# Seven block products instead of eight, also in the down projection of the feed-forward layers

## The chip, the cores and the metric

The kernel runs on one core of one Trainium2 chip. The metric is the device time of one launch in microseconds (us), as the median of several runs. Lower is better.

## The reference, cut to what matters

The program is a two-layer decoder trunk on 256 tokens of width 2048, all in float32. The change touches only the feed-forward part, which each of the two layers has once:

```python
D_MODEL = 2048; SEQ = 256; FFN_HIDDEN = 5632
def swiglu(xn, w_gu, w_down):          # xn (256, 2048), w_gu (2048, 11264), w_down (5632, 2048)
    g, u = jnp.split(xn @ w_gu, 2, axis=-1)
    return (jax.nn.silu(g) * u) @ w_down
...
h = h + swiglu(rms_norm(h, ffn_norm_g[layer]), ffn_w_gu[layer], ffn_w_down[layer])
```

## The kernel before

**Numbers.** TensorE multiplies in a reduced float32 format. So every operand is kept as two tiles, a rounded `hi` and the rest `lo`, and every product of two blocks is three matmuls: x-hi by w-hi, x-hi by w-lo, x-lo by w-hi. A weight block comes from HBM as a `raw` tile. ScalarE (ACT) casts it to `hi`, VectorE (DVE) subtracts and gives `lo`. This is done by the class `WeightStream`: one call of `ws.next()` hands out the unit that TensorE (PE) multiplies now, emits the split of the unit two places ahead, and the loads of the three units after that. There are three buffers of `raw`, three of `hi` and three of `lo`. SyncE (SP) issues the loads.

**Units.** A unit is 128 x 2048 weights. In the gate and up projection a unit is two row blocks (128 inputs each) by two column blocks of 512, one of gate and one of up; eight units in a row (`kp` 0 to 7) make one pass over the 2048 inputs, for 512 hidden columns. In the down projection a unit is four row blocks by one column block of 512, multiplied by `x_stationary`. Either way a unit of the plain kind ("eight") is 8 block products of 128 x 128 by 128 x 512, which with three matmuls each is 24 matmuls for both halves of the tokens.

**Seven products.** In a gate and up pass the units `kp` 2, 4 and 6 (`SEVEN`) are done by a Strassen-like scheme. A unit is a 2 by 2 matrix of weight blocks, and the tokens and inputs that it meets are a 2 by 2 matrix of 128 x 128 blocks. Sums and differences of blocks on both sides make the product in 7 block products, so 21 matmuls. The price is on the other engines. On the weights (`split_blocks`): one cast and one subtraction of 1536 columns instead of 2048, four sums of 512 columns in place (L184 to L187), and a second split of all four sums into `th` and `tl`. There is one buffer of `th` and of `tl`. On the inputs (`forms`): sums of blocks of x, made once per layer, since the same x meets all gate and up columns. On the output: four products are gathered in four PSUM banks `pb` over the three units; after the last of them DVE joins them with four additions (L707).

**Accumulators.** PSUM has two accumulators `acc` of two banks each, and four single banks. A gate and up pass takes both accumulators, and all four banks from `kp` 2 to 6. The next pass may write its first accumulator when DVE has added the old one into `gate` (L711). In the down projection one pass (512 output columns) takes one accumulator, so two passes alternate.

**Order.** The 5632 hidden columns are worked in three parts of 16, 16 and 12 blocks of 128 (`FFN_PARTS`). In each part, a gate and up pass for every 512 hidden columns, silu and product, and then the transposition of the result into `hT`: eight PE transposes, put into `hT` as hi and lo. That work is queued with `later.put(1, ...)`, so it lands behind the first unit of the next pass. After the gate and up passes of a part come its four down passes (512 output columns each), added into the residual stream `h` (L734). Each engine has a queue that it works off in order; the place of each instruction in it is fixed when the kernel is built.

In the text below, B0 to B7 are the eight units of a gate and up pass, and D0, D1, ... the units of a down pass.

Of the kernel before, what the change touches and what calls it, by code (L numbers as in the profile page):

```python
# [47 lines left out]
SEVEN = (2, 4, 6)  # L48

# [172 lines left out]
def kernel(ctx, tc, consts, x, attn_norm_g, ffn_norm_g, a_w_qkv, a_w_o, kv_norm_g,  # L222
# [411 lines left out]
    def ffn(xT, rstd, finish):  # L634

        with tc.tile_pool(name="ffn", bufs=1) as fp:
# [9 lines left out]
            forms = fp.tile([P, len(SEVEN), 2, 4, P], F32R, name="forms")  # L646

            def scaled(kp):

                x2 = xT[:, 2 * kp:2 * kp + 2, :].rearrange("p k (h s) -> p k h s", s=S)  # L650
                by = row["R"].unsqueeze(1).unsqueeze(1).broadcast_to([P, 2, 2, S])
                nc.vector.tensor_tensor(out=x2, in0=x2.bitcast(F32), in1=by, op=ALU.mult)
                if kp not in SEVEN:
                    return
                f = tmp.tile([P, 2, S], F32, tag="t1", name="f")
                nc.vector.tensor_tensor(out=f, in0=x2[:, :, 0, :].bitcast(F32), in1=x2[:, :, 1, :].bitcast(F32),
                                        op=ALU.add)
                (a11, a21), (a12, a22) = [[f[:, k, t * P:(t + 1) * P] for t in range(NT)] for k in range(2)]
                g = tmp.tile([P, 4, P], F32, tag="t1", name="g")
                for i, x, y, op in ((0, a21, a22, ALU.add), (1, g[:, 0], a11, ALU.subtract),  # L660
                                    (2, a11, a21, ALU.subtract), (3, a12, g[:, 1], ALU.subtract)):
                    nc.vector.tensor_tensor(out=g[:, i], in0=x, in1=y, op=op)
                d = forms[:, SEVEN.index(kp)]
                put_split(d[:, 0], d[:, 1], g)

            def mixed(seven, gate, up):
# [3 lines left out]
                ga, ua = acc_tile(), acc_tile()  # L670
# [8 lines left out]
                for kp in range(KD // 2):  # L679
                    w = ws.next()  # L680
                    x = lambda t, kk: [xT[:, 2 * kp + kk, o + t * P:o + (t + 1) * P] for o in (0, S)]
                    if seven and kp in SEVEN:
                        i = SEVEN.index(kp)
                        st, sp = i == 0, i == len(SEVEN) - 1
                        if st:
                            pb = [bank() for _ in range(4)]
                        y = lambda j: [forms[:, i, h, j, :] for h in range(2)]
                        mul(pb[0], x(0, 0), w[:2], 1, st, sp)
                        mul(ga[:, 0], x(0, 1), w[:2], 3, False, False)
                        mul(ua[:, 0], y(3), w[:2], 2, False, False)  # L690
                        mul(ga[:, 1], x(1, 1), w[2:], 3, False, False)
# [3 lines left out]
                    else:  # L695
                        st, sp = kp == 0, kp == KD // 2 - 1
                        for acc, n in ((ga, 1), (ua, 0)):
# [4 lines left out]
                    if seven and kp == SEVEN[-1]:  # L702
                        u2 = fp.tile([P, 512], F32, tag="u2", name="u2")
                        nc.scalar.copy(out=gate[:, 0], in_=pb[0])
                        for o, x_, y_ in ((u2, pb[2], gate[:, 0]), (gate[:, 1], pb[3], u2),
                                          (up[:, 0], pb[1], u2), (up[:, 1], pb[1], gate[:, 1])):
                            nc.vector.tensor_tensor(out=o, in0=x_, in1=y_, op=ALU.add)  # L707
                if not seven:
                    return ga, ua
                for acc, d in ((ga, gate), (ua, up)):  # L710
                    nc.vector.tensor_tensor(out=d, in0=acc, in1=d, op=ALU.add)  # L711
                return gate, up

            for part, (k0, n) in enumerate(FFN_PARTS):
                last = part == len(FFN_PARTS) - 1
                hT = big_tile([P, 16, 2 * S], F32R, "hT")
                for j in range(0, n, 4):
                    gate, up = [fp.tile([P, NT, 512], F32, tag=m, name=m) for m in ("gate", "up")]
# [4 lines left out]
                    g, u = mixed(not first, gate, up)  # L723
# [3 lines left out]
                    for t in range(NT):  # L727
                        nc.vector.scalar_tensor_tensor(out=up[:, t], in0=u[:, t], scalar=sc_[:, t:t + 1],
                                                       in1=gate[:, t], op0=ALU.mult, op1=ALU.mult)
                    later.put(1, lambda j=j, up=up, hT=hT:  # L730
                              transposed([up[:, t, :] for t in range(NT)], hT, j, None))

                def add(acc, c, t):
                    nc.vector.tensor_tensor(out=chunk(t, c), in0=acc[:, t, :], in1=chunk(t, c), op=ALU.add)  # L734
                    if last:
                        finish(c, t)

                for c in range(4):
# [201 lines left out]
```

## Time and profile before

| | |
|---|---|
| median of 3 runs | 2680.39 us (2678.89 to 2680.82) |
| the profiled execution's own time | 2679.5 us |
| its span, first to last instruction | 2677.7 us |
| TensorE busy | 2661.3 us, 12986 matmuls and transposes |
| VectorE busy | 1915.4 us |
| ScalarE busy | 1264.4 us |
| HBM read | 491.57 MB, 184 GB/s over the span |

The profile lists for each engine the instructions with start and duration, what they waited for, and the chain of work that ended last. A matmul's listed duration overlaps with the next one's; how often one starts tells the rate. The same holds for VectorE in a smaller measure: back-to-back instructions start a little before the one ahead is listed as ended, so the work of a queue is summed by the distance of starts.

### The profile page before, as it was taken

What the parts mean: (1) busy time and instruction counts of PE and PEld (TensorE: products, weight loads), DVE (VectorE), ACT (ScalarE), POOL (GpSimd) and SP (SyncE); (2) the same over time, 40 slices, a digit from 0 to 9 for tenths busy, and PEclk for the clock granted to TensorE, in tenths of its full rate; (3) what the DMA queues carried; (4) which work ended last, traced back from release to release, by engine and by line L of the source; (5) the groups of instructions that cost most, each with busy time, mean ns of one, the idle gap of its engine ahead of it and who ended that gap; (6) DMA issues with size and microseconds to landing.
All of it is one profiled execution on the core that took longest, in us unless ns stands there. A gap on an engine that the chain in (4) does not pass through costs nothing.

```text
span 2677.7 us, 32660 instructions
## 1 busy us (share of the span) xinstructions
PE 2661.3 (99%) x12986; PEld 2236.9 (84%) x12986; DVE 1915.4 (72%) x2584; ACT 1264.4 (47%) x1603; POOL 5.5 (0%) x12
## 2 busy tenths in 40 slices
PE   9999999999999999999999999999999999999998
PEld 7888888888888888888888888888888888888887
DVE  5676577477467668966995796588578848984985
ACT  5444444444444445544553454565445534543553
POOL 0000000000000000000000000000000000000000
PEclk9999999999999999999999999999999999999999
DMA  7545555555555555565565655544555665655564
GB/s 272 189 160 171 189 165 168 186 173 173 173 183 164 195 182 189 189 204 189 189 219 190 204 180 197 161 140 146 174 173 189 205 198 179 219 190 194 191 217 138
DMA packets 302712, 495.78 MB, mean 185 GB/s; under 512 B 12680, under 2 KB 115808, under 8 KB 302176
## 3 DMA queue, kind: packets, MB, share of 16 engines
q1 hardware_dynamic: 301936, 492.64, 55.4%
q8 instruction: 101, 1.65, 0.3%
q10 hardware_dynamic: 624, 1.07, 0.1%
q14 instruction: 51, 0.42, 0.0%
HBM read 491.57 MB, written 2.10 MB: 184 GB/s over the span
## 4 chain that ended last, share of the span: by engine, by line
PE 95%; DVE 2%; DMA 1%; ACT 1%; issue 1%; SPq 0%; POOL 0%; POOLq 0%; DVEq 0%; ACTq 0%
PE acc L444 14%; PE acc L464 12%; PE acc L463 12%; PE acc L465 12%; PE acc L675 9%; PE acc L676 9%; PE acc L677 9%; PE acc L447 7%; PE bank L676 2%; PE bank L675 2%; PE bank L677 2%; PE bank L398 1%; PE bank L559 1%; DMA raw<-in_ffn_w_gu_dram 1%; PE bank L514 1%
## 5 line engine op out<-in xcount | busy, mean ns | idle before, releaser
L157 DVE TENSOR_TENSOR lo<-raw,hi 128x1024 fp32r<-128x1024 f32 (+2 forms) x578 | 667.5, 1179 | 464.2 <-ACT hi L156 447.9
L156 ACT CAST hi<-raw 128x1024 fp32r<-128x1024 f32 (+2 forms) x578 | 561.6, 1017 | 728.0 <-PE acc L465 312.1
L166 ACT CAST hi<-raw 128x1024 fp32r<-128x1024 f32 (+1 forms) x292 | 323.3, 1139 | 317.8 <-PE acc L677 96.3
L167 DVE TENSOR_TENSOR lo<-raw,hi 128x1024 fp32r<-128x1024 f32 (+1 forms) x292 | 383.4, 1330 | 83.5 <-ACT hi L166 82.8
L675 PE MATMUL acc<-hi,xT_f 128*128 128x512 f32 x988 | 387.2, 392 | 1.7 <-DVE gate L711 1.6
L676 PE MATMUL acc<-lo,xT_f 128*128 128x512 f32 x988 | 385.3, 390 | 0.0
L677 PE MATMUL acc<-hi,xT_f 128*128 128x512 f32 x988 | 385.2, 390 | 0.0
L444 PE MATMUL acc<-xT_a,hi 128*128 128x512 f32 x1536 | 379.3, 395 | 0.0
L444 PEld LDWEIGHTS acc<-xT_a,hi 128*128 128x128 f32 x1536 | 281.5, 188 | 53.8
L463 PE MATMUL acc<-hi,hT 128*128 128x512 f32 x704 | 274.7, 390 | 0.0
L465 PE MATMUL acc<-hi,hT 128*128 128x512 f32 x704 | 274.0, 389 | 0.0
L464 PE MATMUL acc<-lo,hT 128*128 128x512 f32 x704 | 274.0, 389 | 0.0
L675 PEld LDWEIGHTS acc<-hi,xT_f 128*128 128x128 f32 x988 | 185.5, 188 | 42.5 <-issue 2.9
L677 PEld LDWEIGHTS acc<-hi,xT_f 128*128 128x128 f32 x988 | 185.5, 188 | 39.3
L676 PEld LDWEIGHTS acc<-lo,xT_f 128*128 128x128 f32 x988 | 185.5, 188 | 38.4
L447 PEld LDWEIGHTS acc<-xT_a,lo 128*128 128x128 f32 x1536 | 196.9, 191 | 7.6
L447 PE MATMUL acc<-xT_a,lo 128*128 128x256 f32 x1536 | 199.2, 283 | 0.0
L166 ACT CAST th<-raw 128x1024 fp32r<-128x1024 f32 x120 | 121.8, 1049 | 73.1 <-DVE raw L186 64.6
L463 PEld LDWEIGHTS acc<-hi,hT 128*128 128x128 f32 x704 | 132.2, 188 | 27.6 <-issue 0.2
L465 PEld LDWEIGHTS acc<-hi,hT 128*128 128x128 f32 x704 | 132.1, 188 | 27.6
L464 PEld LDWEIGHTS acc<-lo,hT 128*128 128x128 f32 x704 | 132.2, 188 | 26.9
L464 PE MATMUL acc<-lo,xT_a 128*128 128x512 f32 x384 | 150.1, 391 | 0.8 <-DVE lo L157 0.6
(222 smaller groups left out, 3539.9 us busy)
## 6 DMA issues: line engine op xcount, KB each, us to landing
raw<-in_ffn_w_gu_dram SPq DMA_DIRECT2D x352, 512.0 KB, 4.5
raw<-in_a_w_qkv_dram SPq DMA_DIRECT2D x143, 1024.0 KB, 4.8
raw<-in_ffn_w_down_dram SPq DMA_DIRECT2D x88, 1024.0 KB, 5.1
raw<-in_a_w_o_dram SPq DMA_DIRECT2D x16, 1024.0 KB, 5.1
raw<-in_b_w_o_dram SPq DMA_DIRECT2D x16, 1024.0 KB, 5.0
raw<-in_b_w_kv_b_dram SPq DMA_DIRECT2D x8, 1024.0 KB, 5.2
raw<-in_b_w_q_b_dram SPq DMA_DIRECT2D x8, 768.0 KB, 4.8
raw<-in_b_w_q_a_dram SPq DMA_DIRECT2D x4, 1024.0 KB, 5.1
```

Of the source, the lines that this page charges most:

```text
L156: nc.scalar.copy(out=h, in_=src)
L157: nc.vector.tensor_tensor(out=l, in0=src, in1=h.bitcast(F32), op=ALU.subtract)
L166: self.nc.scalar.copy(out=hi, in_=src)
L167: self.nc.vector.tensor_tensor(out=lo, in0=src, in1=hi.bitcast(F32), op=ALU.subtract)
L444: mm(out=acc[:, i, :], lhsT=sl(hi, kk), rhs=xT[:, k0 + kk, :], start=first and kk == 0, stop=False)
L447: mm(out=acc[:, i, 0:S], lhsT=sl(lo, kk), rhs=xT[:, k0 + kk, 0:S], start=False, stop=last and kk == nk - 1)
L463: mm(out=acc[:, t, :ncol], lhsT=xh, rhs=rhs(hi, kk), start=st, stop=False)
L464: mm(out=acc[:, t, :ncol], lhsT=xh, rhs=rhs(lo, kk), start=False, stop=False)
L465: mm(out=acc[:, t, :ncol], lhsT=xl, rhs=rhs(hi, kk), start=False, stop=sp)
L675: mm(out=out, lhsT=xh, rhs=wh, start=st, stop=False)
L676: mm(out=out, lhsT=xh, rhs=wl, start=False, stop=False)
L677: mm(out=out, lhsT=xl, rhs=wh, start=False, stop=sp)
```

## The change

The seven-product scheme is now used in the down projection too. Two down passes are joined into one over 1024 output columns, whose units are two row blocks by two column blocks, like those of gate and up. In the two parts of 16 blocks this is done for all four passes (two joined passes of 8 units, seven-product units 2 and 5); in the last part, of 12 blocks, for the first 1024 columns (one joined pass of 6 units, seven-product units 2 and 4), while its last two passes stay as they were. That makes 4 + 4 + 2 = 10 seven-product units per layer, 20 in all.

The gate and up loop is generalised: `mixed` takes the input tile, the list of seven-product units and the sums. `sums` makes the block sums of the inputs; for the down projection it runs on `hT`, behind the transposition that completes the blocks concerned, into a new tile `forms_h`. To make room, `forms` keeps three of four sums; the fourth is written over a block of x that the scheme doesn't read. `joined` adds the joined products into `h`, and each accumulator is then added into `h` on its own.

```diff
+SEVEN_DOWN = {16: (2, 5), 12: (2, 4)}
...
-            for c in range(0, D, 512):
+            v = ffn_w_down[layer].rearrange("(k p) c -> p k c", p=P)
+            last = k0 + n == KF
+            for c in range(0, 1024 if last else D, 1024):
+                for kp in range(n // 2):
+                    blocks = [v[:, k0 + 2 * kp:k0 + 2 * kp + 2, b:b + 512] for b in (c, c + 512)]
+                    units.append((blocks, None, "seven" if kp in SEVEN_DOWN[n] else "eight"))
+            for c in range(1024 if last else D, D, 512):
                 for k in range(k0, k0 + n, 4):
                     add_unit(ffn_w_down[layer], k, 4, c, 512)
...
-            forms = fp.tile([P, len(SEVEN), 2, 4, P], F32R, name="forms")
+            forms = fp.tile([P, len(SEVEN), 2, 3, P], F32R, name="forms")
+            forms_h = fp.tile([P, 2, 2, 4, P], F32R, name="forms_h")
+            def sums(x, kp, d):
+                x2 = x[:, 2 * kp:2 * kp + 2, :].bitcast(F32)
+                f = tmp.tile([P, 2, S], F32, tag="t1", name="f")
+                nc.vector.tensor_tensor(out=f, in0=x2[:, :, 0:S], in1=x2[:, :, S:2 * S], op=ALU.add)
+                (a11, a21), (a12, a22) = [[f[:, k, t * P:(t + 1) * P] for t in range(NT)] for k in range(2)]
+                g = tmp.tile([P, 4, P], F32, tag="t1", name="g")
+                for i, x_, y_, op in ((0, a21, a22, ALU.add), (1, g[:, 0], a11, ALU.subtract),
+                                      (2, a11, a21, ALU.subtract), (3, a12, g[:, 1], ALU.subtract)):
+                    nc.vector.tensor_tensor(out=g[:, i], in0=x_, in1=y_, op=op)
+                if d.shape[2] == 3:
+                    put_split(x[:, 2 * kp, P:S], x[:, 2 * kp, S + P:2 * S], g[:, 0])
+                    g = g[:, 1:]
+                put_split(d[:, 0], d[:, 1], g)
...
-            def mixed(seven, gate, up):
+            def mixed(X, pairs, seven, sums_of, left, right, joined=None):
...
-                    later.put(1, lambda j=j, up=up, hT=hT:
-                              transposed([up[:, t, :] for t in range(NT)], hT, j, None))
+                    def turned(j=j, up=up, hT=hT, seven=SEVEN_DOWN[n]):
+                        transposed([up[:, t, :] for t in range(NT)], hT, j, None)
+                        for kp in (j // 2, j // 2 + 1):
+                            if kp in seven:
+                                sums(hT, kp, forms_h[:, seven.index(kp)])
+                    later.put(1, turned)
+                for c in range(0, 2 if last else 4, 2):
+                    left, right = pair_tiles()
+                    cols = [h[:, :, (c + i) * 512:(c + i + 1) * 512] for i in range(2)]
+                    def joined(cols=cols, parts=(left, right)):
+                        for d, p in zip(cols, parts):
+                            nc.vector.tensor_tensor(out=d, in0=p, in1=d, op=ALU.add)
+                    accs = mixed(hT, n // 2, SEVEN_DOWN[n], forms_h, left, right, joined)
+                    for i, acc in enumerate(accs):
+                        for t in range(NT):
+                            nc.vector.tensor_tensor(out=chunk(t, c + i), in0=acc[:, t, :], in1=chunk(t, c + i),
+                                                    op=ALU.add)
...
-                for c in range(4):
+                for c in range(2 if last else 4, 4):
```

How the queues change is seen best on VectorE, at three places. Names carry a running number of the tile; `lo` and `tl` rows are the second halves of weight splits, `raw` rows the four weight sums of a seven-product unit.

**Place 1: the end of the third part's first down pass** (first layer). Before, on VectorE: the additions into `h` are from an accumulator that alternates with another, and stand between weight splits.

```order
L157 TENSOR_TENSOR lo_12183<-raw_12068,hi_12182 128x1024
L817 MEMSET qz01_13087 64x256
L816 MEMSET qz10_13088 64x256
L817 MEMSET qz11_13089 64x256
L157 TENSOR_TENSOR lo_12215<-raw_12103,hi_12214 128x1024 x2
L734 TENSOR_TENSOR h_7143<-acc_12135,h_7143 128x512 x2
L157 TENSOR_TENSOR lo_12256<-raw_12142,hi_12255 128x1024 x2
```

After, on VectorE: from the join of D4 (the last seven-product unit) to the end of D5 (the last unit of the joined pass).

```order
L158 TENSOR_TENSOR lo_12494<-raw_12394,hi_12493 128x1024 x2
L724 TENSOR_TENSOR u2_12522<-bank_12438,gate_12320 128x512
L158 TENSOR_TENSOR lo_12531<-raw_12434,hi_12530 128x1024
L724 TENSOR_TENSOR gate_12320<-bank_12439,u2_12522 128x512
L724 TENSOR_TENSOR up_12321<-bank_12437,u2_12522 128x512
L724 TENSOR_TENSOR up_12321<-bank_12437,gate_12320 128x512
L766 TENSOR_TENSOR h_7143<-gate_12320,h_7143 128x2x512
L766 TENSOR_TENSOR h_7143<-up_12321,h_7143 128x2x512
L158 TENSOR_TENSOR lo_12531<-raw_12434,hi_12530 128x1024
L771 TENSOR_TENSOR h_7143<-acc_12322,h_7143 128x512 x2
L771 TENSOR_TENSOR h_7143<-acc_12323,h_7143 128x512 x2
```

The rows L771 on `acc_12322` free the accumulator that TensorE's next pass writes first; they now stand behind the join, two additions of 1024 columns and two halves of splits.

**Place 2: a gate and up pass whose `hT` blocks need sums** (the third pass of the first part, first layer), from the `hT` rows to the weight sums of B4. Before, on VectorE:

```order
L374 TENSOR_TENSOR hT_7627<-bank_8325,hT_7627 128x2x256
L167 TENSOR_TENSOR lo_8333<-raw_8204,hi_8332 128x1024
L167 TENSOR_TENSOR lo_8366<-raw_8240,hi_8365 128x1536
L184 TENSOR_TENSOR raw_8240<-raw_8240 128x512
L185 TENSOR_TENSOR raw_8240<-raw_8240 128x512
L167 TENSOR_TENSOR lo_8408<-raw_8291,hi_8407 128x1024
L186 TENSOR_TENSOR raw_8240<-raw_8240 128x512
```

After, on VectorE:

```order
L381 TENSOR_TENSOR hT_7628<-bank_8332,hT_7628 128x2x256
L662 TENSOR_TENSOR f_8339<-hT_7628 128x512
L168 TENSOR_TENSOR lo_8349<-raw_8211,hi_8348 128x1024
L667 TENSOR_TENSOR g_8341<-f_8339 128x128 x2
L667 TENSOR_TENSOR g_8341<-g_8341,f_8339 128x128
L168 TENSOR_TENSOR lo_8382<-raw_8247,hi_8381 128x1536
L667 TENSOR_TENSOR g_8341<-f_8339,g_8341 128x128
L185 TENSOR_TENSOR raw_8247<-raw_8247 128x512
L168 TENSOR_TENSOR lo_8424<-raw_8298,hi_8423 128x1024
L381 TENSOR_TENSOR forms_h_7627<-g_8341,forms_h_7627 128x512
L186 TENSOR_TENSOR raw_8247<-raw_8247 128x512
L168 TENSOR_TENSOR lo_8424<-raw_8298,hi_8423 128x1024
```

Six instructions of the sums (one `f`, four `g`, one `forms_h`) stand between the splits of B3, B4 and B5.

**Place 3: the end of a gate and up pass** (the last of the third part, first layer, where B6 is the last seven-product unit), on VectorE. Before:

```order
L157 TENSOR_TENSOR lo_12098<-raw_12007,hi_12097 128x1024
L707 TENSOR_TENSOR u2_12091<-bank_11938,gate_11827 128x512
L157 TENSOR_TENSOR lo_12098<-raw_12007,hi_12097 128x1024
L707 TENSOR_TENSOR gate_11827<-bank_11939,u2_12091 128x512
L707 TENSOR_TENSOR up_11828<-bank_11937,u2_12091 128x512
L707 TENSOR_TENSOR up_11828<-bank_11937,gate_11827 128x512
L711 TENSOR_TENSOR gate_11827<-acc_11829,gate_11827 128x1024
```

After, on VectorE, at the same place:

```order
L168 TENSOR_TENSOR lo_12246<-raw_12147,hi_12245 128x1024 x2
L724 TENSOR_TENSOR u2_12275<-bank_12118,gate_11998 128x512
L168 TENSOR_TENSOR lo_12282<-raw_12188,hi_12281 128x1024
L724 TENSOR_TENSOR gate_11998<-bank_12119,u2_12275 128x512
L724 TENSOR_TENSOR up_11999<-bank_12117,u2_12275 128x512
L724 TENSOR_TENSOR up_11999<-bank_12117,gate_11998 128x512
L168 TENSOR_TENSOR lo_12282<-raw_12188,hi_12281 128x1024
L744 TENSOR_TENSOR gate_11998<-acc_12000,gate_11998 128x1024
```

One half of a split more stands between the first join row and the addition that frees the first accumulator. This order is found at 4 of the 20 ends of such passes, twice in each layer; at 2 more, the first such end of each layer, both halves stand between the last join row and that addition; at the other 14 the order is that of before.

More of the change, by code (lines that the diff above doesn't have):

```diff
@@ L652, in scaled @@
                 nc.vector.tensor_tensor(out=x2, in0=x2.bitcast(F32), in1=by, op=ALU.mult)
[L653 to L664, printed above, removed]
-            def mixed(seven, gate, up):
-                ga, ua = acc_tile(), acc_tile()
+                if kp in SEVEN:
+                    sums(xT, kp, forms[:, SEVEN.index(kp)])
+            def mixed(X, pairs, seven, sums_of, left, right, joined=None):
+                la, ra = acc_tile(), acc_tile()
                 pb = None
@@ L677, in mul @@
                     mm(out=out, lhsT=xl, rhs=wh, start=False, stop=sp)
[L679 removed]
+                for kp in range(pairs):
                     w = ws.next()
[L681 to L684, printed above, removed]
+                    x = lambda t, kk: [X[:, 2 * kp + kk, o + t * P:o + (t + 1) * P] for o in (0, S)]
+                    if kp in seven:
+                        i = seven.index(kp)
+                        st, sp = i == 0, i == len(seven) - 1
                         if st:
                             pb = [bank() for _ in range(4)]
[L687 removed]
+                        o4 = sums_of.shape[3] - 4
+                        y = lambda j: x(1, 0) if j + o4 < 0 else [sums_of[:, i, h, j + o4, :] for h in range(2)]
                         mul(pb[0], x(0, 0), w[:2], 1, st, sp)
[L689 to L691 removed]
+                        mul(la[:, 0], x(0, 1), w[:2], 3, False, False)
+                        mul(ra[:, 0], y(3), w[:2], 2, False, False)
+                        mul(la[:, 1], x(1, 1), w[2:], 3, False, False)
                         mul(pb[1], y(0), w[2:], 0, st, sp)
@@ L695, in mixed @@
                     else:
-                        st, sp = kp == 0, kp == KD // 2 - 1
-                        for acc, n in ((ga, 1), (ua, 0)):
+                        st, sp = kp == 0, kp == pairs - 1
+                        for acc, n in ((la, 1), (ra, 0)):
                             for t in range(NT):
@@ L701, in mixed, with pair_tiles @@
                     later.tick()
-                    if seven and kp == SEVEN[-1]:
+                    if seven and kp == seven[-1]:
                         u2 = fp.tile([P, 512], F32, tag="u2", name="u2")
-                        nc.scalar.copy(out=gate[:, 0], in_=pb[0])
-                        for o, x_, y_ in ((u2, pb[2], gate[:, 0]), (gate[:, 1], pb[3], u2),
-                                          (up[:, 0], pb[1], u2), (up[:, 1], pb[1], gate[:, 1])):
+                        nc.scalar.copy(out=left[:, 0], in_=pb[0])
+                        for o, x_, y_ in ((u2, pb[2], left[:, 0]), (left[:, 1], pb[3], u2),
+                                          (right[:, 0], pb[1], u2), (right[:, 1], pb[1], left[:, 1])):
                             nc.vector.tensor_tensor(out=o, in0=x_, in1=y_, op=ALU.add)
[L708 to L712, printed above, removed]
+                        if joined:
+                            joined()
+                return la, ra
+            def pair_tiles():
+                return [fp.tile([P, NT, 512], F32, tag=m, name=m) for m in ("gate", "up")]
             for part, (k0, n) in enumerate(FFN_PARTS):
@@ L717, in ffn @@
                 for j in range(0, n, 4):
-                    gate, up = [fp.tile([P, NT, 512], F32, tag=m, name=m) for m in ("gate", "up")]
+                    gate, up = pair_tiles()
                     first = k0 + j == 0
@@ L722, in ffn @@
                             later.put(kp + 3, lambda kp=kp: scaled(kp))
-                    g, u = mixed(not first, gate, up)
+                    g, u = mixed(xT, KD // 2, () if first else SEVEN, forms, gate, up)
+                    if not first:
+                        for acc, d in ((g, gate), (u, up)):
+                            nc.vector.tensor_tensor(out=d, in0=acc, in1=d, op=ALU.add)
+                        g, u = gate, up
                     sc_ = rstd if first else rem
```

6 lines of the change are left out of this document (4 added, 2 removed).

## The prediction

> **What bounds the kernel.** I read the page's busy shares first, then the slices, the chain of work that ended last, and a table of stages.
>
> ```profile
> span 2677.7 us, 32660 instructions
> PE 2661.3 (99%) x12986; PEld 2236.9 (84%) x12986; DVE 1915.4 (72%) x2584; ACT 1264.4 (47%) x1603; POOL 5.5 (0%) x12
> ...
> DVE  5676577477467668966995796588578848984985
> ...
> PEclk9999999999999999999999999999999999999999
> ...
> PE 95%; DVE 2%; DMA 1%; ACT 1%; issue 1%; SPq 0%; POOL 0%; POOLq 0%; DVEq 0%; ACTq 0%
> ```
>
> TensorE is busy 99% of the span at full clock and carries 95% of the chain: a matmul that goes away is time won, as long as no one else is late. VectorE's 72% is an average: the slices reach 9. The table of stages shows which those are (columns: stretch, length, then busy us of PE, PEld, DVE, ACT, POOL).
>
> ```profile
> 1151.50:1240.00 88.50, 88.50 (x396) 73.37 (x395) 45.58 (x45) 34.23 (x35) 0.00 (x0) 1.00 0.57 186
> ...
> 1283.00:1326.00 43.00, 43.00 (x194) 35.46 (x193) 39.54 (x43) 23.05 (x24) 0.00 (x0) 1.00 0.58 196
> ```
>
> The first is the down stage of part one: VectorE works 45.6 of 88.5 us. The second is one gate and up pass with three seven-product units: VectorE works 39.5 of 43. So the change buys TensorE time with VectorE time, and part of the bill (the sums on `hT`) comes due in the passes where VectorE has 8% left.
>
> **Gain.** Starts of units on TensorE: B3, B4, B5 of one pass; then the first row and the end of 15 units of a down stage.
>
> ```profile
> 1296.79 0.39 PE L675 MATMUL acc<-hi,xT_f 128*128 128x512 f32 x1
> 1302.25 0.39 PE L675 MATMUL bank<-hi,xT_f 128*128 128x512 f32 x1
> 1307.08 0.39 PE L675 MATMUL acc<-hi,xT_f 128*128 128x512 f32 x1
> ...
> 1156.73 0.48 PE L463 MATMUL acc<-hi,hT 128*128 128x512 f32 x1
> ...
> 1238.44 0.39 PE L675 MATMUL acc<-hi,xT_f 128*128 128x512 f32 x1
> ```
>
> A plain unit takes 1302.25 - 1296.79 = 5.46 us, a seven-product unit 1307.08 - 1302.25 = 4.83, a down unit (1238.44 - 1156.73)/15 = 5.45. Rearranging a down unit keeps its 24 matmuls, so it costs TensorE nothing; each of 20 seven-product units saves 5.45 - 4.83 = 0.62 us. Gain: **-12.4 us** if nothing waits.
>
> **Place 1, the end of the third part's joined pass (2 times).** TensorE's next pass needs the first accumulator. The same join is in the trace, at the end of a gate and up pass: B7 starts at 1317.36, the next pass at 1322.83.
>
> ```profile
> 1317.36 0.39 PE L675 MATMUL acc<-hi,xT_f 128*128 128x512 f32 x1
> ...
> 1322.83 0.39 PE L675 MATMUL acc<-hi,xT_f 128*128 128x512 f32 x1
> ```
>
> VectorE meanwhile (in brackets: idle before it and who ended that):
>
> ```profile
> 1316.38 1.23 DVE L167 TENSOR_TENSOR lo<-raw,hi 128x1024 fp32r<-128x1024 f32 x1 [0.19 <-ACT hi L166]
> 1317.52 0.68 DVE L707 TENSOR_TENSOR u<-bank,gate 128x512 f32<-128x512 f32 x1
> 1318.12 1.22 DVE L167 TENSOR_TENSOR lo<-raw,hi 128x1024 fp32r<-128x1024 f32 x1
> 1319.26 0.68 DVE L707 TENSOR_TENSOR gate<-bank,u 128x512 f32<-128x512 f32 x1
> ...
> 1321.24 1.23 DVE L711 TENSOR_TENSOR gate<-acc,gate 128x1024 f32<-128x1024 f32 x1
> ...
> 1173.36 0.69 DVE L734 TENSOR_TENSOR h<-acc,h 128x512 f32<-128x512 f32 x1 [1.99 <-PE acc L465]
> 1173.97 0.68 DVE L734 TENSOR_TENSOR h<-acc,h 128x512 f32<-128x512 f32 x1
> ```
>
> The accumulator is free at 1322.47 and needed at 1322.83, a slack of 0.36 us. In the third part's joined pass the last seven-product unit is D4 of six, so again one plain unit (5.47 us) follows. VectorE's queue there: from `u2` to the end of the joins 3.72 us (1317.52 to 1321.24), two additions of 1024 columns (no such row: by distance of splits, 1318.12 to 1319.26, 1.14 each, plus 0.1 since the second needs a join) 2.4, half a split 1.14, two additions from the accumulator 0.61 + 0.68 = 1.29: 8.55 us. `u2` starts between 0.5 before the unit's end (it reads the third of the four gathered products; only the fourth, three matmuls, lies behind that) and 0.16 after (as in the row). TensorE waits 8.55 - 5.47 = 3.1, less 0.5 or plus 0.16: 2.6 to 3.2. I take 3.0, since the queue ahead of `u2` is short there, but not empty. **+6.0 us** (5.2 to 6.5). In the parts of 16 blocks two plain units follow the last seven-product unit, 10.9 us: the queue is done some 0.7 us ahead, so these four joined passes per layer cost nothing; that cover gone, each would cost what the lateness exceeds 0.7.
>
> **Place 3, an end with half a split more (4 times).** 3.72 + 1.14 + 1.23 = 6.09 us against 5.47, from a `u2` 0.5 early to 0.16 late: 0.1 to 0.8 us each. I take 0.55, for `hi` of that split decides and its cast is late after sums: **+2.2 us** (0.4 to 3.2).
>
> **The first such end of each layer (2 times).** The waits of TensorE on the weights and on `gate` (times: total, count, longest):
>
> ```profile
> PE acc L675 <- DVE gate L711: 1.6, 2, 1.3
> ...
> PE acc L676 <- DVE tl L167: 0.6, 1, 0.6
> ```
>
> The 1.6 us are these two ends. There `u2` waits for a half split whose load is late; in the new order it runs ahead of both halves: 0.60 + 3 joins (about 1.9) + 2.27 + 1.23 = 6.0 against 5.47, so 0.0 to 0.7 each instead of 0.8. **-0.8 us** (-1.6 to 0).
>
> **Place 2, sums in the way of B4's weights (12 times: five gate and up passes and one joined pass a layer).** TensorE needs the second `tl` of B4 at its eleventh matmul. That, VectorE's rows ahead of it, and the ScalarE rows that feed them:
>
> ```profile
> 1304.55 0.39 PE L676 MATMUL acc<-tl,xT_f 128*128 128x512 f32 x1
> ...
> 1293.73 1.76 DVE L167 TENSOR_TENSOR lo<-raw,hi 128x1536 fp32r<-128x1536 f32 x1 [0.29 <-ACT hi L166]
> 1298.31 1.22 DVE L167 TENSOR_TENSOR lo<-raw,hi 128x1024 fp32r<-128x1024 f32 x1
> ...
> 1300.58 1.22 DVE L167 TENSOR_TENSOR tl<-raw,th 128x1024 fp32r<-128x1024 f32 x1
> 1301.71 1.22 DVE L167 TENSOR_TENSOR tl<-raw,th 128x1024 fp32r<-128x1024 f32 x1
> ...
> 1296.89 1.05 ACT L166 CAST hi<-raw 128x1024 fp32r<-128x1024 f32 x1 [3.19 <-DMA raw<-in_ffn_w_gu_dram]
> ...
> 1298.80 1.05 ACT L166 CAST th<-raw 128x1024 fp32r<-128x1024 f32 x1
> ```
>
> It ends at 1302.93: slack 1.6 us. The sums exist in the trace, made for x:
>
> ```profile
> L656 DVE TENSOR_TENSOR f<-xT_f x6: 684/686/687, 997.1 to 1998.5; 128x512 f32<-128x512 f32 x6
> ...
> L662 DVE TENSOR_TENSOR g<-f x12: 284/288/293, 997.9 to 1999.5; 128x128 f32<-128x128 f32 x12
> ...
> L373 ACT CAST forms<-g x6: 615/622/623, 998.9 to 2000.3; 128x512 fp32r<-128x512 f32 x6
> ...
> L374 DVE TENSOR_TENSOR forms<-g,forms x6: 679/686/687, 1000.3 to 2002.0; 128x512 fp32r<-128x512 f32 x6
> ```
>
> Back to back they take 0.08 less: 0.6 + 4 x 0.2 to 0.3 + 0.6 = 2.0 to 2.4 us of VectorE, of which its present idle 0.29 absorbs some. That is 0.1 to 0.8 over the slack. The cast of `forms_h` (0.62 us) waits for the last `g`, and in some passes stands ahead of B5's cast, which now starts as soon as its load lands (1296.89); VectorE's row 1298.31 then comes up to 1 us late too. So 0 to 1.6 us each; walking the queue in the four orders that occur gives 0.0, 0.15, 0.2 and 0.65, and 0.65 in the joined pass. I take 0.3: **+3.6 us** (0 to 19).
>
> **At nothing.** The in-place sum of x adds 6 pairs of small instructions near each layer's start: about 0.3 us of VectorE in passes where it is the late one, bounds 0 to 0.6 in all, within the -0.8 term. A down unit is now loaded by two issues on SP instead of one:
>
> ```profile
> raw<-in_ffn_w_gu_dram SPq DMA_DIRECT2D x352, 512.0 KB, 4.5
> ...
> raw<-in_ffn_w_down_dram SPq DMA_DIRECT2D x88, 1024.0 KB, 5.1
> ```
>
> That is 76 issues more; a pair of half loads lands as soon as one whole, and three are asked for ahead, so TensorE's work on those covers it; the cover gone, a load shows up at most by its 5 us, in one place. `th` and `tl` are single, but two units at least lie between their uses.
>
> **Sum.** -12.4 + 6.0 + 2.2 - 0.8 + 3.6 = -1.4 us. The profiled execution took 2679.5 us (span 2677.7 and 1.8 around it), so 2678.1; the median of the runs lies 0.9 above it: **2679.0 us**. The change removes TensorE work and gets nearly all of it back as waits on VectorE's queue. This kernel's runs tell changes over about 0.2% (5.4 us) from none.
>
> **A rule that speaks against it.** The rows first:
>
> ```profile
> core 0: 2677.7 us, clock 0.999
> ...
> 2660.00:2677.00 17.00, 9.45 (x42) 7.51 (x40) 5.09 (x12) 2.90 (x6) 1.10 (x2) 0.84 0.33 123
> ```
>
> With waits of at most 1.3 us the clock stays at 0.999; in the last 17 us, where TensorE stands idle 7.55, the mean is 0.84. The waits of 3.0 us at place 1 lie between, and the trace has none of that length. If the clock dropped there by half, matmuls would start every 0.45 us instead of 0.227 until it recovers; for between none and one unit of 5.45 us that is 0 to 5.5 us twice. The Trainium skill (TensorE: Matmul & The Clock Gate, "What's actually happening") says that the clock halves after about one idle window of 3.4 us, which free-runs. By that rule a wait of 3.0 us fits no whole window, and the sum stays; at 3.5 or more it would, by an estimate from that page's 3.4 us, add some 1.7 us each time (one window at half speed). No run here shows it.
>
> **Rivals.** *Full gain:* the two units of look-ahead absorb the sums (place 2 at 0), and the other ends are at their lower bounds: -12.4 + 5.2 + 0.4 - 1.6 = -8.4, so 2672.0 us. For it: every slack above was worked out to a few tenths, and VectorE idles 3.5 us in a pass. Against: its queue is in order, and those idle spells lie behind B4. *Slower:* at place 2 each B4 waits 1.6 us, because the cast of `forms_h` holds up B5's: 12 x 1.6 = 19.2 instead of 3.6, so 2694.6. It decides (over 2685.8) from 0.87 us a pass on. For it: both engines there are strictly in order, and the lost time also delays the loads. Against: only some passes have that cast order. *Clock:* place 1 drops the clock, 2679 to 2690. That fewer matmuls are run at all is no question: the order has 60 rows less on TensorE.
>
> **Chances.** Forecast 0.54 (its own range 2674 to 2685), full gain 0.24, slower 0.16, clock 0.06. A forecast that rests on tenths of slack leaks both ways: I put 0.03 of it on faster; the clock case splits evenly between same and slower. Faster 0.27, same 0.54, slower 0.19. The range of 8 in 10 reaches nearly to the full gain and half way to the slower rival: 2671 to 2689.
>
> **What would show it.** Right: 12926 matmuls; TensorE waiting twice about 3 us for the additions into `h` (L771), four times about 0.5 for `gate` (L744), and some tenths on `tl` in passes with sums. Wrong: no wait at L771 (the accumulators then alternate otherwise), waits on `tl` above 0.87 a pass or none, a granted clock below 0.99, or waits on loads in the down stage.

## The result: 0.23% slower

The changed kernel takes 2686.14 us in the median of 11 runs (2682.35 to 2687.20), the kernel before 2679.80 (2677.85 to 2680.82): a ratio of 1.0023, with a 95% interval of 1.0013 to 1.0032. The forecast was 2679.0 and no change. The profiled execution took 2687.15 us, 7.65 more than the one of before.

The head of the page of the changed kernel: span, busy times, the slices of VectorE and of the clock, the shares of the chain.

```profile
span 2685.3 us, 33030 instructions
...
PE 2657.8 (99%) x12926; PEld 2227.0 (83%) x12926; DVE 2070.3 (77%) x2822; ACT 1302.9 (49%) x1651; POOL 5.5 (0%) x12
...
DVE  5666576477477669988998898588589978998986
...
PEclk9999999999999999999999999999999999999999
...
PE 83%; DVE 8%; DMA 4%; issue 2%; ACT 2%; SPq 0%; POOL 0%; ACTq 0%; DVEq 0%; POOLq 0%
```

The 60 matmuls are gone, and VectorE has 155 us more to do. The line to look at is the chain: TensorE carried 95% of it before and carries 83% now. Twelve per cent of the span, over 300 us, is spent on a path that runs through VectorE, ScalarE and loads, although TensorE stands idle only some 11 us more than before. I read such a chain as a TensorE that ran with its weights just ready, so that any delay there was passed on.

The waits of TensorE, and the two stretches that answer to the table of stages (the down stage of part one, then a gate and up pass with sums on `hT`; columns as there):

```profile
PE acc L691 <- DVE gate L744: 4.7, 9, 2.2
PE acc L691 <- DVE h L771: 3.7, 2, 2.7
PE acc L470 <- DVE h L771: 2.3, 1, 2.3
PE bank L405 <- DVE h L771: 1.7, 1, 1.7
...
PE acc L692 <- DVE tl L168: 0.9, 2, 0.8
```

```profile
1150.05:1237.00 86.95, 85.89 (x380) 70.58 (x381) 72.12 (x76) 41.66 (x43) 0.00 (x0) 1.00 0.55 188
1321.97:1365.15 43.18, 42.93 (x191) 35.09 (x192) 41.09 (x48) 23.71 (x26) 0.00 (x0) 1.00 0.52 181
```

The waits on L470 and L405 are the two third-part ends of place 1 (2.3 and 1.7, where 3.0 each was forecast). The other wait on `h`, 3.7 us at L691, stands at the ends of joined passes in the parts of 16 blocks, which had been put at nothing. The wait on `gate` comes nine times, where the forecast had six, and once it is 2.2 us long.

To see where the time went I added up each stage of the two layers, from the start of its first matmul to the start of the next stage's first. The last stage of a layer takes in what follows it. All figures but the medians are from one profiled execution of each kernel. A ratio is to the kernel before as it ran beside that experiment (medians of 2678.9 to 2679.3 beside e1 to e11). The medians are of 11 executions, but of 4 to 7 for e5, e6, e7, e9 and e10.

| kernel | median, us | ratio to before (95%) | gate and up passes, us | down stages, us |
|---|---|---|---|---|
| before | 2679.80 | | 943.0 | 750.2 |
| changed | 2686.14 | 1.0023 (1.0013 to 1.0032) | 949.6 | 751.4 |
| e1, all 24 products | 2682.18 | 1.0011 (1.0002 to 1.0020) | 943.6 | 750.1 |
| e2, no sums on hT | 2679.08 | 0.9998 (0.9989 to 1.0007) | 943.4 | 747.1 |
| e3, accumulators first | 2675.69 | 0.9988 (0.9979 to 0.9997) | 950.0 | 739.8 |
| e4, slots free sooner | 2680.01 | 1.0000 (0.9991 to 1.0009) | 950.3 | 743.9 |
| e6, sums on GpSimd | 2701.78 | 1.0085 (1.0071 to 1.0099) | 961.2 | 750.6 |
| e7, half of them there | 2691.49 | 1.0052 (1.0038 to 1.0065) | 952.0 | 750.1 |
| e5, as e6, accumulators first | 2691.40 | 1.0046 (1.0034 to 1.0059) | 961.3 | 743.8 |
| e8, e3 and other blocks | 2673.74 | 0.9982 (0.9973 to 0.9991) | 945.1 | 743.7 |
| e9, e3 and f copied | 2671.65 | 0.9971 (0.9960 to 0.9983) | 945.9 | 739.9 |
| e10, both | 2670.46 | 0.9968 (0.9955 to 0.9980) | 942.3 | 740.3 |
| e11, e10, joined parts first | 2678.02 | 0.9994 (0.9985 to 1.0003) | 943.2 | 748.2 |

The down stages should have become 12.4 us shorter and are 1.2 longer; the gate and up passes, in which no matmul changed, are 6.6 longer. Together that is the whole difference of the profiled executions. A median can lie up to 3.4 us from the profiled execution of the same kernel (e8), so stages are compared with stages and medians with medians.

### The profile page after: what moved, and what is told of

Same layout as the page of the kernel before. It is cut to its first block, busy times and chain, and to the rows that moved or that the text cites. A ratio compares the mean times of both kernels' runs of the same rounds, so it can differ in the third digit from the quotient of the medians.

```text
span 2685.3 us, 33030 instructions
## 1 busy us (share of the span) xinstructions
PE 2657.8 (99%) x12926; PEld 2227.0 (83%) x12926; DVE 2070.3 (77%) x2822; ACT 1302.9 (49%) x1651; POOL 5.5 (0%) x12
## 4 chain that ended last, share of the span: by engine, by line
PE 83%; DVE 8%; DMA 4%; issue 2%; ACT 2%; SPq 0%; POOL 0%; ACTq 0%; DVEq 0%; POOLq 0%
PE acc L451 14%; PE acc L691 10%; PE acc L693 10%; PE acc L692 10%; PE acc L454 7%; PE acc L470 7%; PE acc L471 7%; PE acc L472 7%; DVE lo L168 2%; PE bank L691 2%; PE bank L693 2%; PE bank L692 2%; DMA raw<-in_ffn_w_down_dram 2%; DMA raw<-in_ffn_w_gu_dram 2%; DVE tl L168 1%
## 5 line engine op out<-in xcount | busy, mean ns | idle before, releaser
L158 DVE TENSOR_TENSOR lo<-raw,hi 128x1024 fp32r<-128x1024 f32 (+2 forms) x426 | 486.7, 1163 | 325.0 <-ACT hi L157 309.2
L167 ACT CAST hi<-raw 128x1024 fp32r<-128x1024 f32 (+1 forms) x424 | 466.0, 1131 | 424.4 <-PE acc L693 172.2
L157 ACT CAST hi<-raw 128x1024 fp32r<-128x1024 f32 (+2 forms) x426 | 407.9, 1004 | 521.7 <-PE acc L451 309.6
L168 DVE TENSOR_TENSOR lo<-raw,hi 128x1024 fp32r<-128x1024 f32 (+1 forms) x424 | 551.9, 1320 | 102.2 <-ACT hi L167 100.9
L691 PE MATMUL acc<-hi,xT_f 128*128 128x512 f32 x988 | 387.2, 392 | 2.4 <-DVE gate L744 1.4
L167 ACT CAST th<-raw 128x1024 fp32r<-128x1024 f32 x160 | 161.8, 1049 | 151.6 <-DVE raw L187 141.5
L691 PEld LDWEIGHTS acc<-hi,xT_f 128*128 128x128 f32 x988 | 185.5, 188 | 43.8 <-issue 4.8
L168 DVE TENSOR_TENSOR tl<-raw,th 128x1024 fp32r<-128x1024 f32 x160 | 189.8, 1220 | 15.3 <-ACT th L167 15.3
L691 PE MATMUL acc<-hi,hT 128*128 128x512 f32 x468 | 184.9, 395 | 6.1 <-DVE gate L744 3.3
L693 PE MATMUL acc<-hi,hT 128*128 128x512 f32 x468 | 183.5, 392 | 0.0
L692 PE MATMUL acc<-lo,hT 128*128 128x512 f32 x468 | 183.5, 392 | 0.0
L470 PE MATMUL acc<-hi,xT_a 128*128 128x512 f32 x384 | 150.6, 392 | 0.0
L472 PE MATMUL acc<-hi,xT_a 128*128 128x512 f32 x384 | 150.5, 392 | 0.0
```

Of the source, the lines that this page charges most:

```text
L157: nc.scalar.copy(out=h, in_=src)
L158: nc.vector.tensor_tensor(out=l, in0=src, in1=h.bitcast(F32), op=ALU.subtract)
L167: self.nc.scalar.copy(out=hi, in_=src)
L168: self.nc.vector.tensor_tensor(out=lo, in0=src, in1=hi.bitcast(F32), op=ALU.subtract)
L470: mm(out=acc[:, t, :ncol], lhsT=xh, rhs=rhs(hi, kk), start=st, stop=False)
L472: mm(out=acc[:, t, :ncol], lhsT=xl, rhs=rhs(hi, kk), start=False, stop=sp)
```

## The experiments

**What the waits look like.** Waits in the text are, unless a fence shows them, the distance of two matmul starts less the usual 0.227 us; the profile counts from the listed end of the matmul before, which gives 0.16 less. The largest loss is the end of the first joined pass of the second layer's part one. The chain of the changed kernel there (start, length, what; L106 is the issue of a load, `x2` joins two instructions):

```profile
2157.64 1.02 DVE tl L168
...
2158.79 1.23 DVE tl L168
...
2160.03 0.37 SPq L106
...
2160.44 6.07 DMA raw<-in_ffn_w_down_dram
...
2166.61 1.06 ACT hi L167
...
2167.69 1.23 DVE lo L168
2168.92 0.60 DVE u L724
...
2176.98 1.21 DVE h L771 x2
...
2178.33 0.77 PE acc L691
```

Read it upwards. TensorE could go on when the first accumulator had been added into `h`. VectorE came to that late, because `u` started late (its row has it at 2168.83): ahead of it in VectorE's order stands the first half split of the next pass's first unit, and its weights had only just landed. They were asked for late, because the slot for them was free only after both `tl` splits of a seven-product unit, whose weight sums are made in the slot itself. D5 ended at 2164.61, `u` started 4.2 us later, and from `u` to the second addition it is 9.35 us at such ends, against 10.9 us of plain units. TensorE waited 2.8 us.

Three theories came from this. *Sums*: the sums on `hT` fill the gate and up passes, and all else follows. *Loop*: the way of a slot (load, cast, split, sums, `tl`, next load) has become too long. *Tail*: the joined parts' additions ahead of the accumulators' make VectorE's queue at the end too long.

**e1, the rearrangement alone.**

```diff
-SEVEN_DOWN = {16: (2, 5), 12: (2, 4)}
+SEVEN_DOWN = {16: (), 12: ()}
```

Expected: 

> Joined down passes of 1024 columns, loaded in two halves, but all 24 products in every unit: no sums on hT, no joins. All theories put it at the kernel before, 2679 to 2681 us, with 12986 matmuls. If the rearrangement itself (two half loads a unit, both accumulators held to the pass's end, freed by four additions in a row) is what costs, it comes out above 2682.

The stages agree with before to 0.6 us, so half loads and joined accumulators cost nothing that this profile shows. But the profiled execution is the fastest of the eleven, and the median is 3.2 us above before's, with an interval (1.0002 to 1.0020) that just excludes no change. It even lies, by 0.2 us, above the 2682 from which the expectation calls the rearrangement itself a cost. So the rearrangement may cost some 3 us in most executions; no profile here shows where.

**e2, no sums on hT.**

```diff
+            nc.vector.tensor_copy(out=forms_h, in_=h[:, 0, :].rearrange("p (a b c d) -> p a b c d", a=2, b=2, c=4))
...
-                        for kp in (j // 2, j // 2 + 1):
-                            if kp in seven:
-                                sums(hT, kp, forms_h[:, seven.index(kp)])
```

Expected: 

> Leaves out the sums on hT (forms_h is filled once per layer with other numbers, so the product is not the reference's); everything else as changed, 12926 matmuls. Theory 'sums' (the sums alone cause the loss): all of it goes, 2671 to 2674 us. Theory 'loop' (the weights' slots go round too slowly: a slot of a seven-product unit is held until its second tl, then reloaded in 5 to 7 us, and the lateness of a gate and up pass survives to the end of the down pass): the gate and up passes get back their slack, the joined ends lose part of their waits, 2676 to 2680. Theory 'tail' (VectorE's queue from the joins to the additions into h is too long by itself): only the waits on tl and at ends of passes with sums go, about 3 us, so 2683.

7 us less than the changed kernel. The gate and up passes are back at 943.4: what they lost, they lost to the sums. The down stages got back 4.3 of 13.6 us; waits at third-part ends (1.9 and 2.5 us) and at two 16-block ends (0.65 and 1.4) stayed without any sums. At the four ends of first joined passes `u` still starts 1.4 to 2.8 us after D5 ends, behind the same half split. The row and `u` at the place shown above, in e2 (`u` is L725 here):

```profile
2162.77 1.23 DVE L168 TENSOR_TENSOR lo<-raw,hi 128x1024 fp32r<-128x1024 f32 x1 [2.79 <-ACT hi L167]
2163.91 0.68 DVE L725 TENSOR_TENSOR u<-bank,gate 128x512 f32<-128x512 f32 x1
```

So the sums are half of the cause and not all of it.

**e3, accumulators first.**

```diff
-                        if joined:
-                            joined()
...
                             nc.vector.tensor_tensor(out=chunk(t, c + i), in0=acc[:, t, :], in1=chunk(t, c + i),
                                                     op=ALU.add)
+                    joined()
```

Expected: 

> The additions of the joined parts into h (2.4 us of VectorE) stand behind the additions from the accumulators instead of ahead of them. Theory 'tail': the waits at the ends of the joined passes (1.9 and 2.5 in the third parts, 1.2, 0.3 and 2.8 with 1.8 at half clock in the others, 10.5 us in all) fall by up to 2.4 each, 9 us less: 2677. Theory 'loop': the same ends fall, but the additions now delay the next pass's splits, which the loop has no slack for: half of it comes back as waits a few units later, 2680 to 2683. Theory 'sums': no change, 2685 to 2687.

10.4 us less than the changed kernel, and faster than before. The down stages fall by 11.6, to 739.8, and the third-part ends to 0.2 us. The gate and up passes keep their 7 us. What the displaced additions delay did not come back as waits; the loop theory's forecast of that was wrong. In the third parts the calls of `finish` move behind the additions as well; in the first layer, two transpositions of `h` out of these calls are what waited (L405).

**e4, slots free sooner.** `s22` and its like are quarters of the two join tiles, which are free at that time. In the edit six of the 20 seven-product units, the first of each part, keep their sums in the slot; the expectation's four is a miscount.

```diff
-        tt(out=b22, in0=b22, in1=b12, op=ALU.subtract)
+        tt(out=s22, in0=b22, in1=b12, op=ALU.subtract)
...
-            self.halve(th[:, i], tl[:, i], raw[:, i])
+            self.halve(th[:, i], tl[:, i], src[n])
```

Expected: 

> The weight sums of all but four seven-product units of the down stages are written to the two join tiles instead of the raw slot; same instructions and durations, but the slot is free after its last sum, about 4 us earlier than after its second tl. Theory 'loop': the next load starts 4 us earlier and the waits at the joined ends of the 16-block parts (6 us with the half clock) go, and part of those in the third parts: 2678 to 2682. Theories 'tail' and 'sums': no change, 2685 to 2687.

6 us less than the changed kernel, by the same instructions with the same durations. The same place in this kernel, VectorE (`u` is L730, the additions from the accumulators L777 here):

```profile
2159.84 3.61 DVE L168 TENSOR_TENSOR lo<-raw,hi 128x1024 fp32r<-128x1024 f32 x3 [3.08 <-ACT hi L167]
2163.36 0.68 DVE L730 TENSOR_TENSOR u<-bank,gate 128x512 f32<-128x512 f32 x1
...
2172.63 1.29 DVE L777 TENSOR_TENSOR h<-acc,h 128x512 f32<-128x512 f32 x2
```

D5 ends at 2163.33 and `u` starts 0.03 us later instead of 4.2. At all eight 16-block ends it is now between 0.02 early and 0.31 late (in the changed kernel up to 4.2), and TensorE waits at one of them, 0.1 us. So the slot was what made these ends late: the loop theory holds there. The third-part ends keep 1.2 and 1.9 us, for the tail theory. Neither e3 nor e4 touches the gate and up passes.

**e6, e7 and e5, the sums on GpSimd.** GpSimd is idle, so the sums were moved to it: all seven instructions with nothing else changed (e6), the last two of them (e7), all with accumulators first (e5). In the diff of e6, `eng` is GpSimd for the sums on `hT`; the four `g` change in the same way as `f`.

```diff
-                nc.vector.tensor_tensor(out=f, in0=x2[:, :, 0:S], in1=x2[:, :, S:2 * S], op=ALU.add)
+                eng.tensor_tensor(out=f, in0=x2[:, :, 0:S], in1=x2[:, :, S:2 * S], op=ALU.add)
...
+                    eng.tensor_copy(out=d[:, 0], in_=g)
+                    eng.tensor_tensor(out=d[:, 1], in0=g, in1=d[:, 0].bitcast(F32), op=ALU.subtract)
```

Expected of e6: 

> The changed kernel with nothing but the sums on hT moved to GpSimd (their result is used). 'Two queues': as where they were left out, gate and up passes back at 943 to 944 us, some waits at the joined ends left, 2678 to 2680. 'Port': 2683 to 2686.

Expected of e7: 

> Of the sums on hT only the cast and the low half of forms_h go to GpSimd; f and the four g (1.7 us) stay on VectorE. If ScalarE's cast of forms_h, which waits for the last g in front of a weight's cast, is what makes the passes late, nearly all comes back: 2679 to 2680. If it is VectorE's time, about a third does (0.6 of 2.3 us): 2683 to 2685.

Expected of e5: 

> Accumulators first, as before, and all seven instructions of the sums on hT on GpSimd, which is otherwise idle. Theory 'two queues' (the loss is the sums' time on VectorE and ScalarE in the gate and up passes, 6 to 7 us, plus VectorE's queue at the joined ends, 10 to 12 us): both go, 2668 to 2671 us, gate and up passes 943 us in all and down stages 740. Rival 'port' (GpSimd's work slows VectorE's rows beside it by as much as it takes off): the gate and up passes stay near 950 and the time near 2676, with longer mean splits on VectorE in the passes with sums.

All three are worse than anything expected: e6 15.6 us slower than the changed kernel, though VectorE and ScalarE have less to do. GpSimd in one such pass of e6 (idle before in brackets):

```profile
1331.53 2.21 POOL L661 TENSOR_TENSOR f<-hT 128x512 f32<-128x512 f32 x1 [201.04 <-DVE hT L381]
1333.82 2.73 POOL L666 TENSOR_TENSOR g<-f 128x128 f32<-128x128 f32 x2
...
1340.54 1.62 POOL L674 TENSOR_TENSOR forms_h<-g,forms_h 128x512 fp32r<-128x512 f32 x1
```

VectorE in the same pass:

```profile
1329.43 0.69 DVE L187 TENSOR_TENSOR raw<-raw 128x512 f32<-128x512 f32 x1
...
1332.50 3.72 DVE L168 TENSOR_TENSOR tl<-raw,th 128x1024 fp32r<-128x1024 f32 x2
...
1341.04 1.66 DVE L186 TENSOR_TENSOR raw<-raw 128x512 f32<-128x512 f32 x1
...
1346.35 2.35 DVE L168 TENSOR_TENSOR tl<-raw,th 128x1024 fp32r<-128x1024 f32 x2
```

While GpSimd works, from 1331.53 to 1342.16, two `tl` splits take 3.72 us, against 2.35 once it is done; a weight sum takes 1.66 against 0.69. `f` takes 2.21 on GpSimd and 0.68 on VectorE. VectorE loses more than was taken off it (over the whole run it is busy for 2083.6 us with 2750 instructions, against 2070.3 with 2822 in the changed kernel), and TensorE's waits on `tl` in the passes with sums, about 1 us each (1348.75 and 1393.46), follow. The rival 'port' was right in its sign and too small. The Trainium skill (Perfetto Trace Analysis, "Optimizing Scalar/DVE Operations") says that the two engines share a read port and that moving work between them might not help; these rows agree, and show that it can cost. e7, for this reason, does not tell ScalarE's cast from VectorE's time.

**e8, e9 and e10, other blocks and a copied f.** All three have accumulators first. e8 makes the sevens of the 16-block parts from blocks of the last gate and up pass, so that their sums run in the joined pass. e9 lets ScalarE copy `f` from the bank. e10 does both.

```diff
-SEVEN_DOWN = {16: (2, 5), 12: (2, 4)}
+SEVEN_DOWN = {16: (3, 5), 12: (2, 4)}
+ORDER = {16: (0, 1, 2, 6, 3, 7, 4, 5), 12: (0, 1, 2, 3, 4, 5)}
```

```diff
-                nc.vector.tensor_tensor(out=f, in0=x2[:, :, 0:S], in1=x2[:, :, S:2 * S], op=ALU.add)
+                    nc.scalar.copy(out=f, in_=ps)
```

Expected of e8: 

> Accumulators first, and in the parts of 16 blocks the seven-product units are made of the blocks of the last gate and up pass (unit order 0,1,2,6,3,7,4,5, sevens at the fourth and sixth place), so that their sums on hT run in the joined pass, where VectorE works half the time; only one gate and up pass a layer (third part) keeps sums. If the sums cost their time because they stand in full passes, the gate and up passes come back to 944 to 945 us and the down stages stay at 740: 2669 to 2672. If lateness is made anywhere VectorE has more work, the first joined passes get it instead: 2674 to 2676.

Expected of e9: 

> Accumulators first; f is copied from the bank by ScalarE (about 0.6 us of it) instead of added from the two halves of hT by VectorE (0.69 us), 12 times. If VectorE's time is what is missing, 0.6 of its 2.3 us a pass go: 1.5 to 2.5 us less than with accumulators first alone, 2673 to 2674. If ScalarE's place in the order is what is missing, no gain or a loss of up to 3: 2676 to 2679.

Expected of e10: 

> Both of the last two. With sums that cost only in full passes: as the new unit order alone, to within 1 us, 2668 to 2672.

e8 does what was expected in the gate and up passes (945.1) and loses 4 us in the down stages, where sums now push two `tl` of 16-block parts late by 0.4 and 0.6 us and a wait of 2.4 us in the second layer's third part brings a spell at half clock. e9 beats its forecast: 0.6 us off VectorE, twelve times, comes with a gain of 4 us. But it does not tell VectorE's time from ScalarE's place, for it changes both: `f` comes sooner, and so does the cast of `forms_h`. ScalarE in the pass shown above for e6, in e3 and then in e9:

```profile
1340.04 0.62 ACT L380 CAST forms_h<-g 128x512 fp32r<-128x512 f32 x1 [2.63 <-DVE g L667]
1340.57 2.00 ACT L167 CAST hi<-raw 128x1024 fp32r<-128x1024 f32 x2
...
1335.96 0.62 ACT L380 CAST forms_h<-g 128x512 fp32r<-128x512 f32 x1 [0.36 <-DVE g L672]
1338.43 2.00 ACT L167 CAST hi<-raw 128x1024 fp32r<-128x1024 f32 x2 [1.84 <-DMA raw<-in_ffn_w_gu_dram]
```

In e3 the cast of B5's weights follows that of `forms_h` at once; in e9 it waits for its load alone. Which of the two was missing stays open. e10 has both stages where they belong, 942.3 and 740.3, and is the fastest, 0.32% under before (e9 lies 1.2 us above it, which these few executions hardly tell apart). The shares of its chain, from its page, are back on TensorE:

```profile
PE 95%; DVE 2%; DMA 1%; ACT 1%; issue 1%; SPq 0%; POOL 0%; POOLq 0%; DVEq 0%; ACTq 0%
```

**e11, joined parts first again.** e10 with the order of the additions as in the changed kernel.

Expected: 

> The last kernel's unit order and copied f, but the joined parts' additions into h ahead of the accumulators' again. If the order of these additions costs only where the stream of weights is late or one plain unit follows the joins: the two ends of the third parts come back (2.4 us each, 4 to 5 us, 2674 to 2676), the 16-block ends stay free. If the slots freed late by the seven-product units hold up the 16-block ends by themselves: some of those wait 0.5 to 3 us too, 2677 to 2681.

7.6 us more than e10, all in the last down stage of each layer: the third-part ends wait 2.5 and 2.9 us, and each wait is followed by a spell at half clock. Both branches of the expectation missed that part. The 16-block ends wait nowhere, though slots are freed no sooner: the last `tl` of D5 ends 2.7 to 3.9 us before that unit does on TensorE, against 4.6 to 9.2 in the changed kernel.

This does not show that a late slot is harmless. The other unit order gave VectorE another order too: at the four ends of first joined passes, `u` now stands ahead of all splits of the next pass, and starts 0.42 us before the unit ends. The same place in e11, where the unit ends at 2161.07 (`u` is L730 here):

```profile
2157.06 3.49 DVE L169 TENSOR_TENSOR lo<-raw,hi 128x1024 fp32r<-128x1024 f32 x3
2160.65 0.69 DVE L730 TENSOR_TENSOR u<-bank,gate 128x512 f32<-128x512 f32 x1
...
2165.52 4.67 DVE L169 TENSOR_TENSOR lo<-raw,hi 128x1024 fp32r<-128x1024 f32 x4
```

Nor is it a matter of the lead that the passes before have left: in e2 they are as short as in the kernel before, and `u` is late. The rows fit an end that is late by two things together: a slot that comes free late (e4 takes that away) and a split of its next load ahead of `u` (e11 has none at the ends of first passes). No run changes that order alone, so this last step is argued.

The waits of TensorE in e11, and then the stretches behind the two third-part ends (the granted clock is the third column from the end):

```profile
PE acc L474 <- DVE h L777: 2.7, 1, 2.7
PE bank L408 <- DVE h L777: 2.4, 1, 2.4
```

```profile
1653.98:1658.40 4.42, 4.33 (x12) 3.26 (x13) 4.22 (x7) 2.48 (x8) 0.00 (x0) 0.61 0.71 237
2634.16:2637.60 3.44, 3.44 (x9) 2.75 (x10) 3.44 (x6) 1.76 (x6) 0.00 (x0) 0.54 0.87 296
```

## Why the prediction was wrong

**Gain, -12.4: nearly right.** A down stage of a 16-block part without waits takes 85.6 us instead of 87.95 (the second layer's part two in the changed kernel), 0.59 per seven-product unit: -11.8 for twenty.

**Place 1, +6.0: right place, a little too much.** The two ends wait 1.9 and 2.5 us, 4.4 in all, which is under the lower bound of 5.2. `u` starts 0.43 us before the unit's end there, as early as the lower bound had it, and from `u` to the second addition it is 8.2 us (forecast 8.55). e3 takes it away by moving two additions (2.3 us) behind those from the accumulators, e11 brings it back.

**First ends, -0.8: -1.2.** They wait 0.35 us each instead of 1.45 and 0.45.

**Place 2, +3.6: right in sum, not in spread.** The waits on `tl` and `th` in passes with sums add up to about 3.2 us, but 1.8 of them fall on one pass (at 2112.18 and 2113.44), and five of the twelve passes have none. That the sum fits is in part luck. The rival that the cast of `forms_h` makes each B4 wait 1.6 us is out.

**Place 3, +2.2: more than half the harm is missing.** Eight ends wait beside the first ones, not four, 5.7 us in all. The four with half a split more wait 0.4, 0.5, 0.6 and 2.3 us: three are within the bounds. At the last, 2607.65, down weights were asked for late (a load of 6.5 us that starts when `tl` has freed its slot), and a spell at half clock follows. The other four have the order of before and were put at nothing; there `u` itself starts 0.6 to 1.1 us after the unit's end, and they wait 0.3 to 0.7. The slack of each place was taken as if the pass began on time, but a pass with sums has 41.1 of 43.2 us on VectorE and hands its delay to the next. e2 sets the whole effect of the sums on these passes at 6.2 us; places 2 and 3 and the first ends had 4.4.

**The 16-block ends, "cost nothing": the step that failed.** They cost 1.2, 0.3 and 2.8 us and 1.6 us of half clock, 5.9 in all. Two sentences failed together. One took `u` to start at most 0.16 us after the unit's end; at five of the eight ends it starts 1.0 to 4.2 us after, and what exceeds some 1.5 us (10.9 less 9.35) is a wait. The other put the loads at nothing ("three are asked for ahead"). In the kernel before that was true of down stages, whose plain units free a slot after two half splits. A seven-product unit holds its slot for four sums, two casts and two more splits, so three slots in hand no longer mean three loads on the way. The price was in the text, "at most by its 5 us, in one place"; the likelihood was not. That these ends hang on the slot and on the order of the additions is shown: e4 and e3, each by itself, bring them to 0.1 us or none.

**The clock, 0.06: the mechanism was right, the place and the point at which it sets in were not.** Place 1, which had been named for it, kept its clock in the changed kernel; a 16-block end and an end of place 3 lost it. Three stretches of the changed kernel, columns as in the table of stages (the granted clock is the third from the end):

```profile
2178.33:2181.80 3.47, 3.47 (x9) 2.75 (x10) 3.40 (x4) 0.00 (x0) 0.00 (x0) 0.54 0.88 296
2181.90:2185.30 3.40, 3.40 (x17) 2.77 (x16) 2.94 (x4) 2.00 (x2) 0.00 (x0) 1.00 0.00 1
...
2644.22:2647.60 3.38, 3.38 (x15) 2.79 (x16) 3.38 (x6) 1.96 (x7) 0.00 (x0) 1.00 0.83 300
```

After the wait at 2178.33 nine matmuls fit into 3.47 us at a granted clock of 0.54, then 17 into 3.40 at 1.00. The spells at 2178.33 and at 2607.65 cost 1.6 and 1.7 us. That is the price that was worked out, but TensorE had stood idle for only 2.65 and 2.16 us.

**The sum.** Gate and up passes: forecast +4.4, measured +6.6. Down stages: forecast -5.8 (with 0.6 for place 2), measured +1.2. Of those 7.0 the 16-block ends make 5.9, the clock after 2607.65 another 1.7, the smaller gain 0.6, and place 1 gives 1.6 back; 0.4 is spread over smaller gaps. Forecast and outcome differ by 9 us in the profiled executions; the time stayed inside the range, and the forecast of no change was wrong. By the medians the change costs 6.3 us, and e1 leaves up to 3 of them with the rearrangement, which the prediction put at nothing; that part is open.

## What to carry to other kernels

When matmul time is bought with work on another engine, follow the buffers as well as the queues: what keeps a load's slot longer, and which split of that load stands ahead of what TensorE waits for. In a pass where that engine has 5% left, do not count the slack of each place anew, for a delay can live on to the end of the pass. Then put what frees an accumulator ahead of what only adds up, and the extra work where the engine is half idle: that turned 0.23% slower into 0.32% faster here.

## What the hardware showed that was not expected

The half clock sets in earlier than forecast. From the first feed-forward layer to 2660 us, TensorE stood idle for over 2 us twelve times in the profiled executions of all these kernels (2.06 to 3.56 us, from the end of one matmul to the start of the next). Ten times a spell of about 3.5 us at half rate followed, for 1.5 to 1.8 us each; twice, after 2.32 us (the changed kernel at 2644.22) and 3.07 us (e6), none did. After idle times of 1.45 to 1.78 us, seven in number, it never did. The Trainium skill (TensorE: Matmul & The Clock Gate, "What's actually happening") gives one idle window of about 3.4 us as the condition. The length of the spells agrees with that window; the condition does not, for nine of the ten idle times are shorter than it. That two of the twelve went without fits a window that runs on its own, as the same section has it; no run here can show that.

GpSimd's work on the same kind of data slows VectorE's two-input instructions by up to 2.4 times (1.66 against 0.69 us), so an idle GpSimd is no free engine beside a full VectorE.
